# Sample attention rewritten as half-steps that four engines take in program order

## The chip, the cores and the metric

The kernel is one program on one core of a Trainium2 chip. Six queues matter here. PE is the matrix engine (PEld is its loading of weights), DVE, ACT and POOL are the vector, scalar and GpSimd engines, and SP is the queue that issues the transfers between main memory and the core's own memory (SBUF). The metric is the device time of one execution in microseconds (us), as the median of several runs.

## The reference

The reference is one inference step of a two-layer decoder, for a prompt of 1024 tokens and for 8 sample sequences of 8 new tokens each. The change touches one stage of layer 0, the attention of the sample sequences. Each sequence has 2048 cached tokens, in 16 pages of 128 rows that a page table names; a row is a latent vector of 256 numbers and a rotary key of 32. Cut to what matters:

```
def one(args):                      # lax.map over the 8 sample sequences
    c_all  = concat(cached latents (2048 x 256), new latents (8 x 256))
    kr_all = concat(cached rotary keys (2048 x 32), new ones)
    k_nope = rms_norm(einsum('bkc,chd->bkhd', c_all, w_uk), g_k_nope)   # 8 heads x 64
    s = (qn . k_nope + qr . kr_all) * SOFTMAX_SCALE      # masked among the new tokens
    p = softmax(s)                                       # over the 2056 keys
    lat = einsum('bhqk,bkc->bqhc', p, c_all)
    return einsum('bqhc,chv->bqhv', lat, w_uv)
```

Everything is float32. The kernel gets near it by splitting an operand into a rounded high part and a low part (the rest), and using both.

## The kernel before, in words

The program has six stages; the change lies in the third, `sample_attention` (L813 to L1116), which takes about 421 to 787 us of the span. Behind it come the output projection, the multilayer perceptrons and the recurrent layer, which the change leaves as they are.

**One page.** `load` (L826) reads the page's number and issues two transfers on the SP queue: `cp`, the 128 x 256 latents (128 KB, L840), into a ring of 26 buffers, and `kp`, the rotary keys (L841). `transp` (L915) turns two pages at a time: PE transposes them into `cpt`, ACT casts the high part `ch`, DVE takes the low part `cl`. `keys` (L943) makes 12 matmuls into `pk` (L136: six with 256 columns, six with 320). Of the result, ACT squares the keys (`psq`, L954) and copies the 64 raw scores to `s` (L955), and DVE sums the squares per head (`pss`, L956). `ropes` and `ropes2` add the rotary products, `kpt` and `pr`, for four pages at a time.

**Half a sequence (8 pages).** `scale8` (L958) turns the sums of squares into reciprocal roots (`rsqrt`, L109 to L127: `rsx`, a shift `rst`, a first guess `rsr`, then three Newton steps of three operations, all on DVE), multiplies the scores and adds the rotary part.

**One sequence.** `soft0` to `soft3` take the maximum over the keys (`smx`, transposed in `mxt`, `m`, `sdg`, spread by the matmul `mxb`), and then in two halves subtract it (DVE, L999), take the exponent (ACT, L1000), cast it to the weights' high part `ph` (ACT, L1001) and form their low part (DVE, L1002). A reduction `ssm` (DVE, L1004) sums the weights. Then for each page `vsplit` (L1009) splits `cp` into `vh` (ACT) and `vl` (POOL), a ring of four each, and this split is the last reader of the page's `cp` buffer; `latent` (L1018) makes two matmuls into `lat`. `lat3` turns the result, divides by the sum and writes `latT`. The tiles `kpt`, `mxt`, `mxb` and `lo` share one PSUM bank (`msc`, tag "ms").

**What sets the order.** The main loop (L1069) takes two pages at a time. `slot(b - 1, q)` places the softmax and the weighted sum of one sequence between the pages of the next one. The program's order is only a priority, though: the scheduler of the tile framework puts each engine's instructions in the order in which it expects them to become ready. So the first four `vsplit` of a sequence stand far ahead of its softmax, and the first weights of the output projection (`op.weights(0)`, called by `ahead` when 24 pairs of pages are left) are split long before this stage. The semaphores between engines follow from the tiles.

Of the kernel before, what the change touches and what calls it, by code (L numbers as in the profile page):

```python
# [20 lines left out]
P = 128  # L21
# [76 lines left out]

def wcols(g, w, c0, c1, ring):

    return wunit(g, w[:, c0:c1].rearrange("(k p) m -> p k m", p=P), KB, c1 - c0, ring)


def rsqrt(g, out, ss, inv_n, n, p=P):
# [3 lines left out]
    t = g.tiny.tile([P, 64], I32, name="rst", tag="rst")[:p, :n]  # L108
# [13 lines left out]
    v.tensor_single_scalar(t, x.bitcast(I32), 1, ALU.logical_shift_right)  # L122
    v.tensor_scalar(r.bitcast(I32), t, -1.0, float(0x5F3759DF), ALU.mult, ALU.add)
# [142 lines left out]
class OutProj:  # L266
# [47 lines left out]
def in_even(g, I, O, S, st_left):  # L314
# [3 lines left out]
    with ExitStack() as st:  # L318
# [90 lines left out]
        def zproc(ci, tb0, nb, zs, sq):  # L409
# [398 lines left out]
def sample_attention(g, I, S, ahead, fill_start, fill):  # L808
    nc = g.nc
    SQ = H * DT  # L810
    with ExitStack() as st:
# [75 lines left out]
        nc.vector.tensor_copy(i2[NS:], g.ident[NS:, NS:])  # L887
        latT = sa.tile([P, 2, H, NS], F32, name="latT", bufs=1)
# [68 lines left out]

        def scale8(b, g8):  # L958
            ss = ss8[b].rearrange("p a h -> p (a h)")
            r = g.tiny.tile([P, 64], F32, name="prs", tag="prs", bufs=2)  # L960
            rsqrt(g, r, ss, 1.0 / QN, 64)
# [6 lines left out]
        mxs, ph_, sm_, pl_ = {}, {}, {}, {}  # L968
# [22 lines left out]

        def soft3(b, dg):
            s = sc[b]
            pb = msc("mxb")
            nc.tensor.matmul(pb[:, :SQ], g.ones[:SQ], dg[:SQ], start=True, stop=True)
            ph = sa.tile([P, NPG + 1, 2, SQ], F32R, name="ph", tag="ph", bufs=1)
            for x, y in HF:
                sv = s[:, x:y]
                nc.vector.tensor_tensor(sv, sv, pb[:, None, :SQ].to_broadcast([P, y - x, SQ]), ALU.subtract)  # L999
                nc.scalar.activation(sv, sv, AF.Exp, scale=SCALE)  # L1000
                nc.scalar.copy(ph[:, x:y, 0], sv)  # L1001
                nc.vector.tensor_tensor(ph[:, x:y, 1], sv, ph[:, x:y, 0].bitcast(F32), ALU.subtract)  # L1002
# [6 lines left out]
        def vsplit(b, pg):  # L1009
            ch = sa.tile([P, R], F32R, name="vh", tag="vh", bufs=4)  # L1010
            c_l = sa.tile([P, R], F32R, name="vl", tag="vl", bufs=4)
            nc.scalar.copy(ch, cps[b, pg])
            e = nc.vector if b == DB - 1 and pg % 4 else nc.gpsimd
            e.tensor_tensor(c_l, cps.pop((b, pg)), ch.bitcast(F32), ALU.subtract)
            vs[b, pg] = (ch, c_l)

        def latent(b, pg):
# [9 lines left out]
            nc.tensor.matmul(pl[:, :R], w, vh, start=(pg == 0), stop=False)  # L1027
# [4 lines left out]
        def lat2(b):  # L1032
            ls = sa.tile([P, R], F32, name="ls", tag="ls")
            nc.scalar.copy(ls, pl_.pop(b)[:, :R])
            lss[b] = ls

        def lat3(b):
            ls = lss.pop(b)
            po = msc("lo")
            for k in range(2):  # L1040
                nc.tensor.matmul(po[:, k * SQ:(k + 1) * SQ], ls[:, k * P:(k + 1) * P], i2, start=True, stop=True)
            nc.tensor.matmul(po[:, 2 * SQ:3 * SQ], g.ones, sm_.pop(b), start=True, stop=True)
            ri = sa.tile([P, SQ], F32, name="sri", tag="sri")
            nc.vector.reciprocal(ri, po[:, 2 * SQ:3 * SQ])
            for k in range(2):
                nc.vector.tensor_tensor(latT[:, k, :, b * DT:(b + 1) * DT], po[:, k * SQ:(k + 1) * SQ].rearrange("p (h t) -> p h t", t=DT),
                                        ri.rearrange("p (h t) -> p h t", t=DT), ALU.mult)

        def slot(b, q):

            if b < 0:
# [5 lines left out]
            if 3 <= q <= 11:  # L1057
                for pg in range(2 * (q - 3), min(2 * (q - 3) + 2, NPG)):
                    vsplit(b, pg)
            if 5 <= q <= 13:  # L1060
                for pg in range(2 * (q - 5), 2 * (q - 5) + 2):
                    if pg <= NPG:
                        latent(b, pg)
            if q == 13:
                lat2(b)
            if q == 15:
                lat3(b)

        st_ = {}  # L1069
# [4 lines left out]
        for J in range(NJ + 8):  # L1074
            b, pr = divmod(J, 8)
            if J == NJ:
                stk.close()
                fill_start()
            if J < NJ:
                ahead(NJ - J)  # L1080
                if J + 2 < NJ:
                    load(*divmod(J + 2, 8))
                if pr == 0 and b > 0:
                    scale8(b - 1, 1)
                    soft1(b - 1)
                if pr == 4:
                    scale8(b, 0)
                    soft0(b)
# [529 lines left out]
```

## Time and profile before

| what | us |
|---|---|
| median of three runs | 2800.52 (2797.41 to 2801.54) |
| the profiled execution | 2799.98 |
| its span | 2798.1 |
| PE busy | 2694.8 (96%) |
| DVE busy | 1779.9 (64%) |
| ACT busy | 899.4 (32%) |
| POOL busy | 364.4 (13%) |

The span goes from the first to the last instruction. A row of a timeline gives when an instruction began and how long it took, and in brackets how long its engine had been idle before and what released it; an "x4" joins four neighbours that are alike. PE's matmuls overlap, so that their spacing, not their duration, tells what they cost. A clock of 1.00 is TensorE's full 2.4 GHz, 0.50 is 1.2 GHz.

### The profile page before, as it was taken

How to read it: one execution, taken by the hardware profiler on the slowest of the kernel's cores; microseconds unless marked ns; L12 is line 12 of the kernel's file. 1: busy time of each engine (PE TensorE's matmuls, PEld its weight loads, DVE VectorE, ACT ScalarE, POOL GpSimd, SP SyncE). 2: the span in 40 equal slices, each digit the busy share in tenths (PEclk: the TensorE clock that was granted, in tenths of full speed). 3: DMA queues.
4: the chain of work that ended last, by engine and by line, in shares of the span. 5: the costliest groups of instructions: out<-in, count | busy, mean ns of one | idle time of the engine just before them, and what ended most of it. 6: DMA issues, size and time to landing. Idle time of an engine off the chain costs nothing.

```text
span 2798.1 us, 42984 instructions
## 1 busy us (share of the span) xinstructions
PE 2694.8 (96%) x16801; PEld 2612.2 (93%) x16801; DVE 1779.9 (64%) x3477; ACT 899.4 (32%) x1878; POOL 364.4 (13%) x429
## 2 busy tenths in 40 slices
PE   7998999999899999999999999998999999999999
PEld 6887988888889999999999989998999999999998
DVE  7665666888855555555555577996555555555555
ACT  5334555666644111111111135664411111111111
POOL 4221000332322000000000033444200000000000
PEclk9999998999999999999999999999999999999999
DMA  5233103221251111111111111113111111111111
GB/s 156 63 117 109 39 9 80 67 56 50 61 147 51 46 39 49 43 46 46 46 46 46 46 73 45 42 41 110 56 40 45 46 46 46 46 46 46 38 31 65
DMA packets 200742, 162.06 MB, mean 58 GB/s; under 512 B 40331, under 2 KB 183148, under 8 KB 199763
## 3 DMA queue, kind: packets, MB, share of 16 engines
q1 hardware_dynamic: 200539, 159.31, 19.1%
q8 instruction: 133, 2.18, 0.3%
q14 instruction: 70, 0.57, 0.1%
HBM read 138.18 MB, written 21.21 MB: 57 GB/s over the span
## 4 chain that ended last, share of the span: by engine, by line
PE 63%; DVE 7%; ACT 1%; issue 0%; DMA 0%; POOL 0%; ACTq 0%; DVEq 0%; SPq 0%; POOLq 0%
PE up L136 27%; PE dn L136 26%; PE op L136 6%; PE pu L136 2%; DVE xl L182 1%; DVE v L1339 1%; DVE ig L1354 1%; PE pgt L136 1%; DVE hs L1370 0%; DVE t L1355 0%; DVE y L250 0%; DVE ta L1357 0%; DVE xl L80 0%; PE pg L136 0%; DVE ig L1363 0%
## 5 line engine op out<-in xcount | busy, mean ns | idle before, releaser
L250 DVE TENSOR_TENSOR y<-y,dn 128x384 f32<-128x384 f32 (+1 forms) x768 | 404.6, 530 | 281.9 <-PE dn L136 279.8
L136 PE MATMUL dn<-hh,whB 128*128 128x384 f32 (+1 forms) x1536 | 505.7, 329 | 3.9 <-DVE y L250 3.8
L136 PE MATMUL up<-xh,wlA 128*128 128x384 f32 (+1 forms) x1536 | 501.6, 327 | 0.0
L136 PE MATMUL up<-xh,whA 128*128 128x384 f32 (+1 forms) x1536 | 501.1, 326 | 0.0
L136 PE MATMUL dn<-hh,wlB 128*128 128x384 f32 (+1 forms) x1536 | 501.0, 326 | 0.0
L136 PE MATMUL up<-xl,whA 128*128 128x384 f32 (+1 forms) x1536 | 501.0, 326 | 0.0
L136 PE MATMUL dn<-hl,whB 128*128 128x384 f32 (+1 forms) x1536 | 500.6, 326 | 0.0
L79 ACT CAST whB<-raw 128x1024 fp32r<-128x1024 f32 (+3 forms) x80 | 79.9, 1034 | 701.7 <-PE dn L136 663.2
L136 PEld LDWEIGHTS dn<-hh,whB 128*128 128x128 f32 x1536 | 288.3, 188 | 11.8 <-DVE y L250 11.6
L136 PEld LDWEIGHTS up<-xh,wlA 128*128 128x128 f32 x1536 | 288.3, 188 | 0.4
L136 PEld LDWEIGHTS up<-xh,whA 128*128 128x128 f32 x1536 | 288.3, 188 | 0.3
L136 PEld LDWEIGHTS dn<-hl,whB 128*128 128x128 f32 x1536 | 288.4, 188 | 0.1
L136 PEld LDWEIGHTS up<-xl,whA 128*128 128x128 f32 x1536 | 288.3, 188 | 0.2
L136 PEld LDWEIGHTS dn<-hh,wlB 128*128 128x128 f32 x1536 | 288.3, 188 | 0.0
L235 DVE SCALAR_TENSOR_TENSOR rl<-up,rs 128x384 f32<-128x384 f32 (+1 forms) x192 | 102.8, 535 | 260.4 <-PE up L136 260.4
L236 ACT ACTIVATE hh<-rl 128x384 fp32r<-128x384 f32 (+1 forms) x192 | 97.1, 506 | 447.7 <-DVE rl L235 447.7
L136 PE MATMUL pk<-wqh,cl 128*128 128x256 f32 (+1 forms) x512 | 153.3, 305 | 12.7 <-DVE cl L925 12.6
L79 ACT CAST whA<-raw 128x1024 fp32r<-128x1024 f32 (+2 forms) x94 | 98.0, 1043 | 195.1 <-PE up L136 143.2
L136 PE MATMUL pk<-wqh,ch 128*128 128x320 f32 (+1 forms) x512 | 159.8, 314 | 0.7 <-ACT ch L924 0.7
L80 POOL TENSOR_TENSOR wlA<-raw,whA 128x1024 fp32r<-128x1024 f32 (+2 forms) x24 | 58.1, 2422 | 768.6 <-ACT whA L79 768.6
L237 DVE TENSOR_TENSOR rl<-rl 128x384 f32<-128x384 f32 (+1 forms) x192 | 105.9, 552 | 77.5 <-ACT hh L236 77.5
L136 PE MATMUL pk<-wql,ch 128*128 128x256 f32 (+1 forms) x512 | 151.7, 298 | 1.2 <-DVE wql L80 1.2
(556 smaller groups left out, 5272.4 us busy)
## 6 DMA issues: line engine op xcount, KB each, us to landing
raw<-in_w_up_dram SPq DMA_DIRECT2D x64, 512.0 KB
raw<-in_w_down_dram SPq DMA_DIRECT2D x64, 512.0 KB
cp<-in_cache_ckv_dram SPq DMA_DIRECT2D x128, 128.0 KB
raw<-in_w_in_rnn_dram SPq DMA_DIRECT2D x16, 512.0 KB
xt<-in_x_prompt_dram SPq DMA_DIRECT2D x8, 512.0 KB
raw<-in_w_out_even_dram SPq DMA_DIRECT2D x8, 512.0 KB
raw<-in_x_prompt_dram SPq DMA_DIRECT2D x8, 512.0 KB
raw<-in_w_out_rnn_dram SPq DMA_DIRECT2D x8, 512.0 KB
```

The costliest lines, as they stand in the source:

```text
L79: g.nc.scalar.copy(h, src)
L80: (lo or g.nc.vector).tensor_tensor(l, src, h.bitcast(F32), ALU.subtract)
L136: g.nc.tensor.matmul(ps, a, b, start=(i == 0), stop=(i == n - 1))
L182: nc.vector.scalar_tensor_tensor(xl[:, m], yv, gcol[:, m:m + 1], xh[:, m].bitcast(F32), ALU.mult, ALU.subtract)
L235: nc.vector.scalar_tensor_tensor(r[:, :n], ps[:, :n], 0.0, RS[c][:, :n], ALU.max, ALU.mult)
L236: nc.scalar.activation(hh[:, a:b], r[:, :n], AF.Square)
L237: nc.vector.tensor_tensor(r[:, :n], r[:, :n], r[:, :n], ALU.mult)
L250: nc.vector.tensor_tensor(y[c][:, m], y[c][:, m], ps[:, :n], ALU.add)
L1339: V.scalar_tensor_tensor(v, ul[:, a + k:b + k], vec[:, k, n:n + 1], v, ALU.mult, ALU.add)
L1354: V.scalar_tensor_tensor(t2, t2, 1.0, v, ALU.add, ALU.mult)
```

## The change

The change rewrites the stage in five ways.

1. `rsqrt` makes its first guess in one operation, without the shift, and can put its Newton steps on another engine. `scale8`'s root becomes `norm8`: `rsx` and `rsr` on DVE, and then 12 operations on POOL.
2. The sum of the weights comes out of the weighted sum itself. Each `vh` has two columns of ones behind its 256, so that the high matmul of `latent` has 258. The `ssm` reduction, the matmul with ones and the 128 x 64 reciprocal go; `lat3` has a small matmul `lf` and a reciprocal of one column in their place, and `lat4` does the rest.
3. `vh` and `vl` are four fixed pairs of tiles.
4. The loop goes by half-steps of one page, n, and stands under `manual_schedule` for PE, DVE, ACT and POOL: these take their instructions in the order of the program. Of a sequence's 16 half-steps, the next sequence's half-step q carries the softmax: q = 0 the second `norm8`, 2 `scale8`, 5 `mxt`, 6 `mxb` with the first exponent and both subtractions, 7 the second exponent, 7 to 14 `vsplit` of two pages each, 8 to 15 their `latent`. `transp` stands at the start of each even half-step, for the pair of pages that is used two half-steps later; before it stood half a step behind.
5. `ahead` loads the first weights of the output projection at 24 pairs left and splits them (`op.parts`) at 20.

The diff, cut to its core:

```
-def rsqrt(g, out, ss, inv_n, n, p=P):
+def rsqrt(g, out, ss, inv_n, n, p=P, eng=None):
...
-    v.tensor_single_scalar(t, x.bitcast(I32), 1, ALU.logical_shift_right)
-    v.tensor_scalar(r.bitcast(I32), t, -1.0, float(0x5F3759DF), ALU.mult, ALU.add)
+    v.tensor_scalar(r.bitcast(I32), x.bitcast(I32), -0.5, float(0x5F3759DF), ALU.mult, ALU.add)
+    if eng is not None:
+        for it in range(3):
+            eng.tensor_tensor(u, r, r, ALU.mult)
+            eng.tensor_tensor(u, u, x, ALU.mult)
+            eng.tensor_scalar(u, u, -0.5, 1.5, ALU.mult, ALU.add)
+            eng.tensor_tensor(out if it == 2 else r, u, r, ALU.mult)
+        return
...
+        fold = sa.tile([P, 2, NS], F32, name="fold", bufs=1)
+        VT = [(sa.tile([P, R + 2], F32R, name=f"vh{i}", bufs=1), sa.tile([P, R], F32R, name=f"vl{i}", bufs=1)) for i in range(4)]
+        for vh, _ in VT:
+            nc.gpsimd.memset(vh[:, R:].bitcast(F32), 1.0)
...
+        def norm8(b):
+            ss = ss8[b].rearrange("p a h -> p (a h)")
+            r = prs[b] = g.tiny.tile([P, 64], F32, name="prs", tag="prs", bufs=2)
+            rsqrt(g, r, ss, 1.0 / QN, 64, eng=nc.gpsimd)
...
-            sm = sa.tile([P, SQ], F32, name="ssm", tag="ssm")
-            nc.vector.tensor_reduce(sm, s.rearrange("p a q -> p q a"), AX.X, ALU.add)
...
         def vsplit(b, pg):
-            ch = sa.tile([P, R], F32R, name="vh", tag="vh", bufs=4)
-            c_l = sa.tile([P, R], F32R, name="vl", tag="vl", bufs=4)
-            nc.scalar.copy(ch, cps[b, pg])
+            ch, c_l = vs[b, pg] = VT[pg % 4]
+            nc.scalar.copy(ch[:, :R], cps[b, pg])
...
-            nc.tensor.matmul(pl[:, :R], w, vh, start=(pg == 0), stop=False)
+            nc.tensor.matmul(pl[:, :R + 2], w, vh, start=(pg == 0), stop=False)
...
         def lat3(b):
+            pf = msc("lf")
+            nc.tensor.matmul(pf[:, :2], fold.rearrange("p a q -> p (a q)"), lss[b][:, R:], start=True, stop=True)
+            nc.vector.reciprocal(ri, pf[:, 0:1])
+            nc.vector.tensor_scalar_mul(i2s, i2, ri)
...
             if q == 0:
+                norm8(b)
+            elif q == 2:
+                scale8(b, 1)
+            elif q == 3:
+                soft1(b)
+            elif q == 5:
                 st_[b] = soft2(b)
-            elif q == 2:
+            elif q == 6:
                 soft3(b, st_.pop(b))
+                shift(b, 0)
+                weigh(b, 0)
+                shift(b, 1)
+            elif q == 7:
+                weigh_low(b, 0)
+                weigh(b, 1)
+            elif q == 8:
+                weigh_low(b, 1)
...
+            if 8 <= q <= 15:
+                for pg in (2 * q - 16, 2 * q - 15):
+                    latent(b, pg)
+            if 7 <= q <= 14:
+                for pg in (2 * q - 14, 2 * q - 13):
                     vsplit(b, pg)
...
+        with g.tc.manual_schedule(engines={ET.PE, ET.DVE, ET.Activation, ET.Pool}):
+            for n in range(2 * NJ):
+                b, q = divmod(n, 16)
+                if q % 2 == 0:
+                    J = n // 2
+                    ahead(NJ - J)
+                    if J + 2 < NJ:
+                        load(*divmod(J + 2, 8))
+                    if J + 1 < NJ:
+                        transp(*divmod(J + 1, 8))
+                if q % 4 == 3:
+                    kT[b, q // 4] = ropes(b, q // 4)
+                slot(b - 2, q + 16)
+                slot(b - 1, q)
+                if q == 8:
+                    norm8(b)
+                elif q == 10:
+                    scale8(b, 0)
+                elif q == 11:
+                    soft0(b)
+                elif q == 13 and b + 1 < DB:
+                    begin(b + 1)
+                keys(b, q)
...
             if left == 24:
-                op.weights(0)
+                op.load(0)
+            elif left == 20:
+                op.parts()
```

Two places of the order, in the second sequence. The first is PE, where the 27th and 28th page of the stage are transposed; these are the first whose `cp` buffers were used before, by pages 1 and 2. Before, `cp_5910` and `cp_5922` are those pages, and `vh_5948` to `vl_5953` belong to the first sequence's pages 7 and 8:

```order
L136 MATMUL pk_6049<-wql1_4917,ch_5965 128x320
L136 MATMUL pk_6049<-wqh1_4916,cl_5966 128x320
L1027 MATMUL lat_5896<-vh_5948,ph_5760 128x256
L1028 MATMUL lat_5896<-vl_5949,ph_5760 128x256
L1027 MATMUL lat_5896<-vh_5952,ph_5760 128x256
L1028 MATMUL lat_5896<-vl_5953,ph_5760 128x256
L921 MATMUL cpt_6079<-ident_73,cp_5910 128x128 x2
L921 MATMUL cpt_6079<-ident_73,cp_5922 128x128 x2
L136 MATMUL pk_6088<-wqh1_4916,ch_5965 128x256
L136 MATMUL pk_6088<-wql1_4917,ch_5965 128x256
```

After, `cp_5861` and `cp_5873` are the 27th and 28th page, and `vh0` to `vl1` hold the first sequence's pages 1 and 2:

```order
L158 MATMUL pk_5923<-wql1_4892,ch_5803 128x320
L158 MATMUL pk_5923<-wqh1_4891,cl_5804 128x320
L957 MATMUL cpt_5966<-ident_73,cp_5861 128x128 x2
L957 MATMUL cpt_5966<-ident_73,cp_5873 128x128 x2
L1074 MATMUL lat_5976<-vh0_4919,ph_5887 128x258
L1075 MATMUL lat_5976<-vl0_4920,ph_5887 128x256
L1074 MATMUL lat_5976<-vh1_4921,ph_5887 128x258
L1075 MATMUL lat_5976<-vl1_4922,ph_5887 128x256
L158 MATMUL pk_6004<-wqh1_4891,ch_5881 128x256
L158 MATMUL pk_6004<-wql1_4892,ch_5881 128x256
```

The transposes moved ahead of the first two latents' matmuls, where before eight pages' stood ahead of them.

The second is POOL, at the first sequence's end. Before, `vl_5801` to `vl_5857` are the splits of its pages 1 to 4, `vl_5889` and on those behind them, and `s<-snew` copies the scores of the new tokens for a sequence's softmax:

```order
L900 AFFINE_SELECT msk_5089<-msk_5089 64x64
L1014 TENSOR_TENSOR vl_5801<-cp_4813,vh_5800 128x256
L1014 TENSOR_TENSOR vl_5805<-cp_4825,vh_5804 128x256
L1014 TENSOR_TENSOR vl_5853<-cp_4837,vh_5852 128x256
L1014 TENSOR_TENSOR vl_5857<-cp_4849,vh_5856 128x256
L978 COPY s_4948<-snew_4943 64x64
L977 MEMSET s_5578 64x64
L978 COPY s_5578<-snew_4943 64x64
L977 MEMSET s_6343 64x64
L978 COPY s_6343<-snew_4943 64x64
L1014 TENSOR_TENSOR vl_5889<-cp_4968,vh_5888 128x256
L1014 TENSOR_TENSOR vl_5893<-cp_4980,vh_5892 128x256
```

After, pages 1 to 4 are `cp_4788` to `cp_4824`, and `rsu_5987` is the root of the second sequence's first half:

```order
L1018 MEMSET s_4937 64x64
L1019 COPY s_4937<-snew_4932 64x64
L1062 TENSOR_TENSOR vl0_4920<-cp_4788,vh0_4919 128x256
L1062 TENSOR_TENSOR vl1_4922<-cp_4800,vh1_4921 128x256
L1062 TENSOR_TENSOR vl2_4924<-cp_4812,vh2_4923 128x256
L1062 TENSOR_TENSOR vl3_4926<-cp_4824,vh3_4925 128x256
L141 TENSOR_TENSOR rsu_5987<-rsr_5988 128x64
L142 TENSOR_TENSOR rsu_5987<-rsu_5987,rsx_5986 128x64
L143 TENSOR_SCALAR rsu_5987<-rsu_5987 128x64
L144 TENSOR_TENSOR rsr_5988<-rsu_5987,rsr_5988 128x64
```

The four splits moved from ahead of the copy of the scores to behind it, and the root's operations, which DVE had, stand behind them and ahead of the next splits.

## Rows read from the trace of the kernel before

**Rows 1.** Windows: us; busy (count) of PE, PEld, DVE, ACT, POOL; clock, DMA share, GB/s.

```profile
517.30:558.80 41.50, 38.95 (x282) 36.22 (x281) 34.43 (x67) 26.51 (x84) 12.21 (x18) 1.00 0.23 58
```

**Rows 2.** Waits, 475.4 to 762 us: total us, times, longest us.

```profile
POOL vl L1014 <- ACT vh L1012: 178.9, 34, 22.8
...
PEld pk L136 <- DVE cl L925: 16.6, 23, 2.7
PE pk L136 <- DVE cl L925: 12.0, 10, 2.5
...
PEld lat L1028 <- POOL vl L1014: 7.4, 15, 0.9
```

**Rows 3.** Timeline of PE: start us, us, engine, line, operation [idle before].

```profile
560.38 0.28 PE L136 MATMUL pk<-wqh,ch 128*128 128x256 f32 x1
...
561.99 0.60 PE L921 MATMUL cpt<-ident,cp 128*128 128x128 f32 x4
...
564.02 0.28 PE L136 MATMUL pk<-wqh,ch 128*128 128x256 f32 x1
...
581.14 0.28 PE L1027 MATMUL lat<-vh,ph 128*128 128x256 f32 x1
581.26 0.28 PE L1028 MATMUL lat<-vl,ph 128*128 128x256 f32 x1
```

**Rows 4.** DVE in the steady part, then in the last sequence (timeline), then grouped lines.

```profile
528.14 1.34 DVE L999 TENSOR_TENSOR s<-s,mxb 128x512 f32<-128x512 f32 x2
...
536.34 2.93 DVE L122 TENSOR_SCALAR rst<-rsx 128x64 int32<-128x64 int32 x1
...
763.55 0.18 DVE L122 TENSOR_SCALAR rst<-rsx 128x64 int32<-128x64 int32 x1
...
781.75 1.23 DVE L1014 TENSOR_TENSOR vl<-cp,vh 128x256 fp32r<-128x256 f32 x3 [0.41 <-ACT vh L1012]
...
L1004 DVE TENSOR_REDUCE ssm<-s 128x64 f32<-128x1088 f32 x7 | 14.8, 2117 | 0.0
```

**Rows 5.** Timeline of ACT in one softmax.

```profile
529.29 0.62 ACT L1000 ACTIVATE s<-s 128x512 f32<-128x512 f32 x1
...
531.41 0.69 ACT L1001 CAST ph<-s 128x576 fp32r<-128x576 f32 x1
...
532.11 0.71 ACT L1012 CAST vh<-cp 128x256 fp32r<-128x256 f32 x2
```

**Rows 6.** POOL: timeline, then one grouped line (busy us, mean ns).

```profile
255.30 2.36 POOL L80 TENSOR_TENSOR wlA<-raw,whA 128x1024 fp32r<-128x1024 f32 x1 [23.55 <-ACT whA L79]
...
420.42 0.28 POOL L899 TENSOR_SCALAR_AFFINE_SELECT msk<-msk 64x64 f32<-64x64 f32 x1
420.77 0.28 POOL L900 TENSOR_SCALAR_AFFINE_SELECT msk<-msk 64x64 f32<-64x64 f32 x1
...
508.38 1.44 POOL L1014 TENSOR_TENSOR vl<-cp,vh 128x256 fp32r<-128x256 f32 x2 [0.86 <-ACT vh L1012]
532.60 2.63 POOL L1014 TENSOR_TENSOR vl<-cp,vh 128x256 fp32r<-128x256 f32 x3 [22.77 <-ACT vh L1012]
...
L1396 POOL TENSOR_TENSOR y<-q,hs 128x64 f32<-128x64 f32 x8 | 3.9, 488 | 0.0
```

**Rows 7.** Page loads: timeline of the SP queue, and windows around the first.

```profile
533.36 0.33 SPq L840 DMA_DIRECT2D cp<-in_cache_ckv_dram  x1
...
534.46 0.33 SPq L840 DMA_DIRECT2D cp<-in_cache_ckv_dram  x1
...
533.30:534.40 1.10, 0.96 (x7) 0.71 (x5) 1.10 (x2) 1.10 (x4) 1.10 (x3) 1.00 0.00 1
534.40:535.40 1.00, 0.30 (x3) 0.12 (x2) 1.00 (x3) 1.00 (x5) 0.94 (x2) 1.00 0.48 147
```

**Rows 8.** Clock in the last sequence: PE timeline, and the window behind it.

```profile
770.20 0.66 PE L1174 MATMUL xtp<-ident,raw 128*128 128x128 f32 x2 [2.19 <-DMA raw<-in_x_prompt_dram]
...
769.40:776.10 6.70, 5.90 (x26) 5.45 (x27) 2.60 (x6) 3.55 (x7) 0.00 (x0) 0.50 0.50 171
```

More of the change, by code (lines that the diff above doesn't have):

```diff
@@ L96, in wunit, with wload, wparts @@
     return v[1], v[2]
+def wload(g, w, c0, c1):
+    raw = raw_tile(g)[:, :1024]
+    g.nc.sync.dma_start(raw.rearrange("p (a b) -> p a b", b=c1 - c0), w[:, c0:c1].rearrange("(k p) m -> p k m", p=P))
+    return raw
+def wparts(g, raw, ring):
+    pl, nb = g.ring[ring]
+    wh = pl.tile([P, 1024], F32R, name="wh" + ring, tag="wh" + ring, bufs=nb)
+    wl = pl.tile([P, 1024], F32R, name="wl" + ring, tag="wl" + ring, bufs=nb)
+    split(g, wh, wl, raw, g.lo)
+    return tuple(t.rearrange("p (a b) -> p a b", a=KB) for t in (wh, wl))
 def wcols(g, w, c0, c1, ring):
     return wunit(g, w[:, c0:c1].rearrange("(k p) m -> p k m", p=P), KB, c1 - c0, ring)
-def rsqrt(g, out, ss, inv_n, n, p=P):
+def rsqrt(g, out, ss, inv_n, n, p=P, eng=None):
     v = g.nc.vector
     x = g.tiny.tile([P, 64], F32, name="rsx", tag="rsx")[:p, :n]
-    t = g.tiny.tile([P, 64], I32, name="rst", tag="rst")[:p, :n]
     u = g.tiny.tile([P, 64], F32, name="rsu", tag="rsu")[:p, :n]
@@ L276, in weights, with load, parts @@
             self.ws[m] = wcols(self.g, self.w, m * P, (m + 1) * P, self.rings[m])
+    def load(self, grp):
+        self.raw = {m: wload(self.g, self.w, m * P, (m + 1) * P) for m in self.GROUPS[grp]}
+    def parts(self):
+        for m, raw in self.raw.items():
+            self.ws[m] = wparts(self.g, raw, self.rings[m])
     def chunk(self, grp, c):
@@ L966, in scale8 @@
             nc.vector.tensor_tensor(sf, sf, pr8[b].rearrange("p a q -> p (a q)"), ALU.add)
-        mxs, ph_, sm_, pl_ = {}, {}, {}, {}
+        mxs, ph_, pl_ = {}, {}, {}
         HF = ((0, 8), (8, NPG + 1))
@@ L1043, in lat3 @@
[L1043 to L1047, printed above, removed]
+                nc.tensor.matmul(po[:, k * SQ:(k + 1) * SQ], ls[:, k * P:(k + 1) * P], i2s, start=True, stop=True)
@@ new lines, in slot @@
+                shift(b, 1)
[4 more added lines that the diff above has]
+                weigh_low(b, 1)
+            elif q == 16:
+                latent(b, NPG)
+                lat2(b)
+            elif q == 17:
+                lat3(b)
+            elif q == 20:
+                lat4(b)
+            if 8 <= q <= 15:
[3 more added lines that the diff above has]
+                for pg in (2 * q - 14, 2 * q - 13):
+                    vsplit(b, pg)
@@ L1073, in sample_attention @@
         NJ = DB * 8
[L1074 to L1086, printed above, removed]
+        ET = mybir.EngineType
+        with g.tc.manual_schedule(engines={ET.PE, ET.DVE, ET.Activation, ET.Pool}):
[15 more added lines that the diff above has]
+                elif q == 10:
                     scale8(b, 0)
+                elif q == 11:
                     soft0(b)
[L1089 to L1092 removed]
+                elif q == 13 and b + 1 < DB:
+                    begin(b + 1)
+                keys(b, q)
+                if n == 2:
                     new_keys()
[L1094 to L1106 removed]
+                if q % 4 == 0 and n:
+                    bb, qq = divmod(n - 4, 16)
+                    ropes2(bb, qq // 4, kT.pop((bb, qq // 4)))
+            ropes2(DB - 1, 3, kT.pop((DB - 1, 3)))
+        stk.close()
+        fill_start()
+        for q in range(21):
+            slot(DB - 2, q + 16)
+            slot(DB - 1, q)
         fill()
```

85 lines of the change are left out of this document (34 added, 51 removed).

## The prediction

> **What bounds the kernel now.** I read the page first: PE is busy for 96% of the span, but over all stages, so I went to the windows of single sequences. A steady sequence takes 41.5 us, and in it PE is busy for 38.95 us, DVE for 34.4, ACT for 26.5 and POOL for 12.2, at full clock [rows 1]. PE bounds the stage, with small gaps. The list of waits names them: 28.6 us on DVE's low part `cl`, 7.4 on POOL's `vl`, from 475 to 762 us, 6.9 sequences [rows 2]; that is some 5.2 us a sequence. PE's own floor from its timeline: a page's 12 matmuls take 1.61 us, a page with the transposes of two 2.03 [rows 3], so 8 x 3.64 = 29.1; 34 latent matmuls at 0.12 are 4.1 [rows 3]; the rotary, maximum and output matmuls are what remains of 41.5 - 5.2 = 36.3, some 3.1. I take a floor of 36.5.
>
> Why is `cl` late? DVE's timeline shows it: `rst`, a 128 x 64 shift that takes 0.18 us in the last sequence, takes 2.93 in the steady part [rows 4], and meanwhile POOL is splitting pages [rows 6]. `cl` queues behind it.
>
> Two more views matter for what replaces this. POOL waits up to 22.8 us for the next `vh` [rows 2], since four pages of the next sequence are split as soon as the ring is free (508.38) and the fifth only when the weights are there (532.60) [rows 6]. And a page load follows the split that frees its buffer: one is issued at 533.36, 0.76 us after the first of three splits began at 532.60 [rows 6, 7].
>
> **Part by part.** All of it is in the steady sequences, in the starting and last ones, and in `op.parts`.
>
> *Less work on DVE.* Per sequence `ssm` (2.1 us [rows 4]), `rst` and the Newton steps go from an engine that isn't the bound. What they are worth is the 5.2 us of PE's waits; with `cl` made two half-steps ahead they can go entirely. The extra columns of the latents lie between 256 and 320 columns, which PE passes in 0.12 us [rows 3] and (1.61 - 6 x 0.12)/6 = 0.15. I take nothing; up to 17 x 0.03 = 0.5 us a sequence.
>
> *New wait 1, the page ring.* PE's order now has the transposes of pages 27 and 28 (the sequence's pages 11 and 12) at the start of half-step 8, in front of the latents. Their loads need the buffers of the former sequence's pages 1 and 2, and these are released by `vl0` and `vl1` of half-step 7. I follow one sequence from its first page, t = 0. `mxt` waits for POOL's root (see below) and for the shared bank, 0.5 us; PE begins half-step 6 at 13.3, and `mxb` comes out at about 14.4. Behind `cl`, DVE makes the two subtractions in 1.34 us [rows 4], until 16.55. The bank is free only then, so `kpt` of half-step 7 waits 0.9 us, and PE ends half-step 7 at 16.55 + 1.75 = 18.3. ACT, strictly in order, casts the first half until 17.2, squares and copies a page (1.1 us), and then takes the second exponent and cast at 0.69 each [rows 5], until 19.7; then `vh0`, `vh1` at 0.36 each [rows 5], until 20.1 and 20.4. POOL's pair takes 1.44 [rows 6]: `vl0` ends at 20.8, `vl1` at 21.5. The load of page 27 is issued at 20.8, that of 28 1.1 later (533.36, 534.46); nothing moves for 1.0 us after an issue, and 128 KB at 147 GB/s take 0.9 [rows 7], so page 28 lands at 23.9. PE has stood since 18.3: a stall of 5.6, from 4.5 (splits and issues that overlap better) to 6.5. Before, these splits stood at 508.38, ahead of the weights that the one at 532.60 waited for [rows 6]. Queued behind the waiting transposes are the latents and the page's matmuls, so nothing fills the gap.
>
> *New wait 2, the root on POOL.* It is 12 dependent operations on 128 x 64. The trace has no such one in SBUF on an idle POOL; a 64 x 64 select takes 0.28 and its dependent successor begins 0.07 later, and a 128 x 64 product has a mean of 0.49 [rows 6]. 12 x 0.35 = 4.2 from below, 12 x 0.56 = 6.7 from above; I take 4.3, the nearer to the select, since the products' mean lies in a stage where DVE is busy beside them. In half-step 8 it stands between `vl3` and the next four splits: `vl3` ends at 26.2, the root at 30.8, and `vl4`, `vl5` at 32.3. PE, from 24.3 on, makes pages 8 and 9 and reaches the latents of half-step 10 at 29.1: a stall of 3.2, from 1.5 to 5.5. The other root, in half-step 0, is covered by five half-steps of matmuls, to within the 0.5 above.
>
> The Trainium skill speaks here against the change. GPSIMD Engine Reference, section "Engine selection", puts two-input elementwise work on VectorE, since GpSimd is about 2x slower. The trace agrees for the split: 0.41 us on DVE [rows 4] against 0.72 on POOL [rows 6]. By twice DVE's pace the root would take about 5.5, which would add 1.2 a sequence, 8 in all, and make it 2845.
>
> *Sum of a sequence.* 36.5 + 0.5 + 0.9 + 5.6 + 3.2 = 46.7, against 41.5: +5.2. Of the eight sequences, the first has no former one; seven make +36.4.
>
> *The first sequence* has `new_keys` in front of its third page in the strict order, and `kpt` in order: +1, between -1 and +4 from the same half-steps.
>
> *`op.parts`* puts two ACT casts and two POOL splits of 2.36 us [rows 6] into half-step 8 of the sixth sequence, where POOL and ACT are late already: 2 x 2.36 less what the load stall hides, +2, between 0 and 4. Before, they were made at 255 us, beside other work.
>
> *The end* loses `ssm` (2.1) and has its root on POOL as well; PE waits there for loads of `x_prompt` too [rows 8], which hide part of either. I take -2, between -4 and +2.
>
> Sum: 36.4 + 1 + 2 - 2 = +37.4, on 2799.98 of the profiled execution (span 2798.1), which is 0.5 below the median of the runs: **2837**.
>
> **The rivals.**
>
> *A, the pipeline works as drawn.* If splits and loads come in time, only the floor and the bank's 1.4 us are left: 37.9, 3.6 less than before, and seven such sequences with the same +1 give -24: 2776. For it: PE's 5.2 us of waits, and DVE's load, which falls by 2.1 of `ssm` and 3.1 of two `rst` [rows 4] and the Newton steps besides. Against it: page 28 would have to land 5.6 us earlier. It decides if `vl1` ends by about 16 instead of 21.5, which needs ACT or POOL to take the splits ahead of the second exponent; the order forbids it.
>
> *B, only one of the two new waits holds.* If the root on POOL is hidden (faster, or begun in the load's gap), a sequence takes 43.5: +2.0 x 7 + 1 = 2815. If only the root's wait holds, it takes 41.1, and the sum is within 2 us of before.
>
> *C, the clock falls.* In the last sequence PE idled 2.19 us, and the window behind it has a granted clock of 0.50 [rows 8], 1.2 GHz. The new gap of 5.6 is longer. At half clock two pages cost 2 x 1.61 = 3.2 us more; much of it disappears in the wait of half-step 10 that follows. If it doesn't, 1.5 to 3 us a sequence are added: 2848 to 2858. Against it: one wait among many, in a stage that was at 1.00 [rows 1].
>
> **How the numbers follow.** A measurement of this kernel can tell about 0.2%, 5.6 us, from no change. The forecast (2824 to 2850 for its own bounds) has a chance of 0.50, C 0.14, B 0.17 with the root hidden and 0.05 with only the root, A 0.14. Faster are A and none else, 0.14; the same is 0.05, the root alone; slower the rest, 0.81. The range leaves out A at the low end and the last of C and of the bounds at the high end: 2804 to 2862.
>
> **What would show it.** In the changed kernel's windows a steady sequence should take 45 to 48 us, with the same PE work. The waits should have PE `cpt` on the page load with 5 to 6 us, seven times, and `lat` on POOL `vl` with about 3 us, seven times; the waits for `cl` should be gone; POOL's root should take about 4.3 us and SP's loads should wait for `vl0` and `vl1`. If `cpt` doesn't wait, the forecast is wrong in its largest term; if sequences take 37 to 38 us, A holds. A clock under 1.00 from half-step 8 on would be C.

## The result and the profile after

The changed kernel takes 2844.79 us (median; 2839.01 to 2849.84) against 2801.03 for the kernel before in the same job: a ratio of 1.0161, with a 95% interval of 1.0148 to 1.0173. It is slower, by 43.8 us. The forecast was 2837, slower, by way of two new waits in each sequence. Both are in the trace. The profiled execution has a span of 2842.0 us.

The windows of the third and fourth sequence, with the columns of [rows 1], and then the waits of all later sequences:

```profile
515.68:566.26 50.58, 42.38 (x282) 40.00 (x280) 27.55 (x46) 26.45 (x84) 20.03 (x42) 0.90 0.18 48
566.26:615.61 49.35, 41.41 (x282) 39.05 (x280) 27.56 (x46) 26.47 (x85) 20.04 (x43) 0.93 0.18 49
```

```profile
PEld cpt L957 <- DMA cp<-in_cache_ckv_dram: 36.0, 14, 4.4
PE cpt L957 <- DMA cp<-in_cache_ckv_dram: 31.8, 14, 4.1
POOL rsu L141 <- DVE rsr L138: 27.1, 11, 4.2
...
PEld lat L1075 <- POOL vl L1062: 19.9, 17, 2.6
PE lat L1075 <- POOL vl L1062: 16.6, 14, 2.4
```

A sequence took 41.5 us [rows 1] and takes 50.6 and 49.4 here. PE's 12 matmuls a page are the same; DVE is busy for 27.6 us where it was 34.4, and POOL for 20.0 where it was 12.2. The waits for `cl` [rows 2] are gone. In their place PE waits for page loads (`cpt`), 31.8 us, and for POOL's `vl`, 16.6 us, over seven sequences. The granted clock is 0.90 and 0.93, where it was 1.00 (the third figure from the end).

PE's timeline in the third sequence has both waits in their places, half-step 8 and half-step 10:

```profile
529.20 0.30 PE L969 MATMUL kpt<-ident,kp 128*128 128x128 f32 x1 [0.57 <-PE pk L158]
...
530.79 0.31 PE L158 MATMUL pk<-wqh,cl 128*128 128x320 f32 x1
535.11 0.44 PE L957 MATMUL cpt<-ident,cp 128*128 128x128 f32 x2 [4.01 <-DMA cp<-in_cache_ckv_dram]
536.17 0.69 PE L957 MATMUL cpt<-ident,cp 128*128 128x128 f32 x2 [0.63 <-DMA cp<-in_cache_ckv_dram]
...
545.35 0.39 PE L1075 MATMUL lat<-vl,ph 128*128 128x256 f32 x1 [2.36 <-POOL vl L1062]
...
546.48 0.58 PE L1075 MATMUL lat<-vl,ph 128*128 128x256 f32 x1 [0.63 <-POOL vl L1062]
```

It idles from 531.1 to 535.1 and again for 0.6 us until the second page is there, and behind `lat<-vh` it stands 2.36 and 0.63 us. What it waits for is on ACT, POOL and SP:

```profile
530.44 0.72 ACT L1048 ACTIVATE s<-s 128x576 f32<-128x576 f32 x1
531.19 0.67 ACT L1049 CAST ph<-s 128x576 fp32r<-128x576 f32 x1
531.77 0.70 ACT L1060 CAST vh<-cp 128x256 fp32r<-128x256 f32 x2
```

```profile
533.05 0.34 SPq L870 DMA_DIRECT2D cp<-in_cache_ckv_dram  x1
...
534.17 0.33 SPq L870 DMA_DIRECT2D cp<-in_cache_ckv_dram  x1
```

```profile
532.30 1.41 POOL L1062 TENSOR_TENSOR vl<-cp,vh 128x256 fp32r<-128x256 f32 x2 [12.15 <-issue]
537.86 1.95 POOL L1062 TENSOR_TENSOR vl<-cp,vh 128x256 fp32r<-128x256 f32 x2 [4.15 <-ACT vh L1060]
540.18 0.29 POOL L141 TENSOR_TENSOR rsu<-rsr 128x64 f32<-128x64 f32 x1 [0.36 <-DVE rsr L138]
...
544.29 0.32 POOL L144 TENSOR_TENSOR prs<-rsu,rsr 128x64 f32<-128x64 f32 x1
544.57 3.23 POOL L1062 TENSOR_TENSOR vl<-cp,vh 128x256 fp32r<-128x256 f32 x4
```

The second exponent and its cast come first on ACT, then `vh` at 531.77, `vl` at 532.30, the page loads at 533.05 and 534.17, and the transposes at 535.11 and 536.17. The root is on POOL from 540.18 to 544.6, 12 operations in 4.4 us, in front of the next splits. What these waits do to the clock:

```profile
531.68:533.68 2.00, 0.00 (x0) 0.00 (x0) 0.62 (x1) 1.45 (x6) 1.38 (x2) 1.00 0.00 0
535.68:537.68 2.00, 1.51 (x7) 1.51 (x8) 0.17 (x1) 0.78 (x2) 0.00 (x0) 0.50 0.10 21
543.20:545.40 2.20, 0.05 (x1) 0.06 (x1) 1.76 (x3) 0.90 (x3) 1.95 (x6) 1.00 0.00 0
546.50:552.00 5.50, 5.50 (x24) 5.46 (x25) 1.67 (x3) 1.64 (x6) 2.29 (x4) 0.50 0.39 103
```

Each time PE has been idle for 2 us and more (531.68 and 543.20), the clock stands at 0.50 soon after the matmuls resume: for 2 us and more behind the first wait, for 5.5 and more behind the second. Not every sequence shows two such falls. From the second to the seventh the mean clock is 0.89, 0.90, 0.93, 0.93, 0.93 and 0.90, and in the fifth and the sixth it falls once only.

The first copy of scores (`s<-pk`) on ACT marks where a sequence begins. By these marks the 43.9 us between the two spans divide so: the prompt attention and the set-up of the stage -10.8, the first sequence +1.2, the seven others +53.7 (286.5 to 340.2, up to the copy of the last page), the end -1.3; the remaining +1.1 lies ahead of 243 us, in a part with no edit.

### The profile page after: what moved, and what is told of

Its sections match the earlier page's. It is cut to its first block, busy times and chain, and to the rows that moved or that the text cites. A ratio compares the mean times of both kernels' runs of the same rounds, so it can differ in the third digit from the quotient of the medians.

```text
span 2842.0 us, 42942 instructions
## 1 busy us (share of the span) xinstructions
PE 2707.4 (95%) x16801; PEld 2627.9 (92%) x16801; DVE 1724.3 (61%) x3300; ACT 898.4 (32%) x1878; POOL 425.6 (15%) x627
## 4 chain that ended last, share of the span: by engine, by line
PE 62%; DVE 7%; ACT 1%; issue 0%; DMA 0%; POOL 0%; ACTq 0%; DVEq 0%; POOLq 0%; SPq 0%
PE up L158 26%; PE dn L158 26%; PE op L158 6%; PE pu L158 2%; DVE xl L204 1%; PE pgt L158 1%; DVE v L1411 1%; DVE hs L1442 1%; DVE ig L1426 1%; DVE y L272 0%; DVE t L1427 0%; DVE xl L80 0%; PE pg L158 0%; DVE ig L1435 0%; DVE ta L1429 0%
## 5 line engine op out<-in xcount | busy, mean ns | idle before, releaser
L992 DVE TENSOR_REDUCE pss<-psq 128x8 f32<-128x512 f32 x128 | 87.6, 685 | 132.1 <-ACT psq L990 132.0
L158 PE MATMUL pk<-wqh,ch 128*128 128x256 f32 (+1 forms) x512 | 165.6, 323 | 0.0
L158 PE MATMUL pk<-wql,ch 128*128 128x256 f32 (+1 forms) x512 | 158.5, 310 | 0.0
```

Of the source, the lines that this page charges most:

```text
L158: g.nc.tensor.matmul(ps, a, b, start=(i == 0), stop=(i == n - 1))
L992: nc.vector.tensor_reduce(ss8[b][:, pg % 8], sq.rearrange("p f (h d) -> p (f h) d", d=QN), AX.X, ALU.add)
```

## The experiments

The first four ran beside each other, and so did the next four, the next two and the last two. All times are medians of four runs, or ten for e6 and e8; "a sequence" is the mean of the third to the fifth in the profiled execution.

| kernel | total, us | ratio to before (95%) | a sequence, us |
|---|---|---|---|
| before | 2797 to 2801 | | 41.5 |
| after | 2844.8 | 1.0148 to 1.0173 | 49.1 |
| e1, early splits | 2818.6 | 1.0049 to 1.0082 | 45.3 |
| e2, root on DVE | 2815.5 | 1.0037 to 1.0070 | 44.6 |
| e3, both | 2778.2 | 0.9905 to 0.9938 | 39.6 |
| e4, weights early | 2854.0 | 1.0169 to 1.0203 | 48.9 |
| e5, e3 + weights at half-steps 2, 4 | 2773.6 | 0.9895 to 0.9928 | 39.6 |
| e6, order free | 2793.5 | 0.9976 to 0.9995 | 41.2 |
| e7, PE filled | 2828.4 | 1.0092 to 1.0126 | 47.4 |
| e8, before with the new first guess | 2799.8 | 0.9992 to 1.0015 | 42.1 |
| e9, e5 + bank | 2774.3 | 0.9893 to 0.9935 | 39.6 |
| e10, order free, root on DVE | 2763.0 | 0.9856 to 0.9899 | 37.3 |
| e11, e10 + weights late | 2756.2 | 0.9833 to 0.9866 | 37.6 |
| e12, e10 + ssm | 2766.7 | 0.9875 to 0.9912 | 37.7 |

One caution for the few microseconds: up to the first `ptp` of the prompt attention, where no edit reaches, the profiled executions differ by up to 5 us (239.1 in e7, 244.1 in e3). There the column of sequences decides. The kernel before came out at 2797 to 2801 in the jobs, so a difference between kernels of different jobs is good to some 4 us.

**e1: the splits of the first four pages early.**

```
-            if 7 <= q <= 14:
+            if 1 <= q <= 4:
+                vsplit(b, q - 1)
+            if 9 <= q <= 14:
                 for pg in (2 * q - 14, 2 * q - 13):
                     vsplit(b, pg)
```

> The changed kernel, with the splits of a sequence's first four pages moved from half-steps 7 and 8 to half-steps 1 to 4; all else as in the changed kernel. Theory (page ring): the transposes of half-step 8 no longer wait for the page loads (31.8 us of PE's waits now, 4 to 5 a sequence), and the half clock behind that wait goes too; the root on POOL still holds the latents of half-step 10, for about 1.7 us. A sequence falls from 48.9 to about 40, the total to about 2785 (2770 to 2800). Rival (strict order): the stage pays for the strict order of ACT and PE as such, and the wait comes back at the latents of half-step 8 or 10 behind the second exponent; then the total stays above 2825.

The total falls by 26.2 us, a sequence to 45.3. No row of waits has `cpt` on a load any more: the page ring was the cause. But PE now comes to half-step 10 earlier, and finds the root still there. PE in the fourth sequence:

```profile
579.96 0.38 PE L1075 MATMUL lat<-vl,ph 128*128 128x256 f32 x1 [2.85 <-POOL vl L1062]
...
581.09 0.58 PE L1075 MATMUL lat<-vl,ph 128*128 128x256 f32 x1 [0.63 <-POOL vl L1062]
```

```profile
PE lat L1075 <- POOL vl L1062: 28.4, 14, 7.2
```

The wait is 2.85 and 0.63 us, not the 1.7 that I expected, and the clock of that sequence 0.96. The theory holds on the first wait; its number failed on the second, which took 28.4 us of PE over the seven sequences, up from 16.6. Of these, 7.5 us are in the sixth, where `op.parts` stands on POOL as well.

**e2: the root on DVE.** In `norm8` the argument `eng=nc.gpsimd` goes:

```
-            rsqrt(g, r, ss, 1.0 / QN, 64, eng=nc.gpsimd)
+            rsqrt(g, r, ss, 1.0 / QN, 64)
```

> The changed kernel, with the Newton steps of the sample attention's root back on DVE (9 operations in place of POOL's 12), in the same place of the order. Theory: the wait of half-step 10's latents on vl (16.6 us in all, 2 to 3 a sequence) goes, and with it the half clock behind it (up to 3 us in some sequences); the wait on the page loads stays at 4 to 5 us. Total 2815 (2805 to 2830). Rival (the page ring alone matters, the second wait only takes up slack that the first leaves): the total stays within 6 us of 2845.

29.3 us less, as expected:

```profile
PE cpt L957 <- DMA cp<-in_cache_ckv_dram: 32.5, 14, 4.1
PE lat L1075 <- POOL vl L1062: 1.3, 3, 0.5
```

PE waits 1.3 us for `vl` in all, and 32.5 for the loads, as much as before this edit. The rival falls: the second wait is not slack that the first leaves.

**e3: both.**

> Both edits together: first four splits at half-steps 1 to 4, Newton steps on DVE. Theory: neither wait is left, a sequence takes 37.9 (36.5 of matmuls and 1.4 for the shared bank) at full clock, total 2770 (2760 to 2785), below the kernel before. Rival (strict order, or the columns of ones, cost by themselves): a sequence stays above 41.5 and the total above 2800.

66.6 us less than the changed kernel, more than the two alone together (55.4), and 22.6 below the kernel before:

```profile
545.20:584.79 39.59, 38.01 (x282) 36.08 (x280) 31.25 (x65) 26.14 (x84) 12.24 (x18) 1.00 0.25 64
624.40:668.87 44.47, 40.13 (x282) 37.56 (x280) 34.52 (x65) 27.38 (x86) 17.44 (x20) 0.96 0.28 80
```

The clock is at 1.00 again: without the two waits, and the clock behind them, the change is no longer slower than what it replaced. A sequence takes 39.6, not 37.9: PE waits 0.80 us at `mxt`, 0.55 at `kpt` and 0.23 at the first latent, and the 38.0 that are left are more than the floor that I took. Of these, e10 shows 37.3; for the other 0.7 no run shows a cause. The second row is the sixth sequence, the one with `op.parts`: 4.9 us longer.

**e4: the weights split as early as before.**

```
+        ahead(99)
         begin(0)
...
-            if left == 24:
-                op.load(0)
-            elif left == 20:
-                op.parts()
+            if left == 99:
+                op.weights(0)
```

> The changed kernel, with the first weights of the output projection loaded and split where the kernel before does it (about 255 us, at the head of the prompt attention) in place of the sixth sequence. Theory: these transfers and splits delay the prompt attention there, which in the changed kernel ends 6.7 us earlier; the total rises by 6 to 7 us to about 2851. Rival (they are free there, as the prediction took it, and cost 2 us in the sixth sequence): 2843.

9.2 us more. In the profiled executions the stretch from 243 us to the first page is 8.0 us longer. The reason stands in ACT's and PE's timelines; of the kernel before, of the changed one and of e4:

```profile
254.18 1.04 ACT L79 CAST whA<-raw 128x1024 fp32r<-128x1024 f32 x1 [6.08 <-DMA raw<-in_w_out_even_dram]
255.13 1.00 ACT L753 ACTIVATE p<-s,nmx 128x896 f32<-128x896 f32 x1
...
256.27 1.75 PE L764 MATMUL ptp<-ident,p 128*128 128x128 f32 x7 [5.87 <-ACT p L753]
```

```profile
250.22 1.01 ACT L783 ACTIVATE p<-s,nmx 128x896 f32<-128x896 f32 x1 [0.81 <-DVE nmx L781]
```

```profile
254.23 1.04 ACT L79 CAST whA<-raw 128x1024 fp32r<-128x1024 f32 x1 [5.37 <-DMA raw<-in_w_out_even_dram]
255.18 1.00 ACT L783 ACTIVATE p<-s,nmx 128x896 f32<-128x896 f32 x1
```

ACT takes its work in order, and the cast of a weight that is still on its way stands in front of the exponents: 6.08 us of waiting, and PE idle for 5.87 behind it. In the changed kernel the exponent of 255.13 begins at 250.22.

**e5: the same weights, in e3, one each at half-steps 2 and 4 of the sixth sequence.**

```
-            elif left == 20:
-                op.parts()
+            elif left in (23, 22):
+                op.parts(23 - left)
```

> Early splits and Newton steps on DVE, as in the run before, and the split of the output projection's first weights moved from half-step 8 of the sixth sequence to its half-steps 2 and 4 (one weight each), where POOL has little to do. Theory: that sequence took 44.5 us where its neighbours take 39.6, with 2.4 us of PE's wait on vl behind POOL's 5.2 us of weights and a half clock after it; it falls to 39.6, the total from 2778 to 2773. Rival (the splits cost what they cost, wherever they stand): 2778.

The total is the theory's, the reason isn't. In the profiled execution the sixth sequence still takes 44.8 us; what is gained lies in the stretch ahead of 240 us (239.6 here, 244.1 in e3). Against the kernel before of its own job, e5 is 24.1 us faster and e3 22.6, so that only some 1.5 of the 4.6 us are left. The rival holds. PE now waits 4.17 us at `mxt`, behind DVE. DVE and POOL, in order of time:

```profile
624.42 1.91 DVE L1005 TENSOR_TENSOR s<-s,prs 128x512 f32<-128x512 f32 x1
...
628.09 2.34 POOL L80 TENSOR_TENSOR wlA<-raw,whA 128x1024 fp32r<-128x1024 f32 x1
...
628.77 2.42 DVE L1022 TENSOR_TENSOR smx<-smx 128x64 f32<-128x64 f32 x1
```

A maximum of 128 x 64 with two inputs takes 0.22 us where POOL is idle (747.83), 0.81 beside a page's split of 0.74 (547.87), and 2.42 beside POOL's split of a weight, and then ends 0.8 us behind it. The product ahead of it takes 1.91 in place of 0.68. The Trainium skill states this for such operations (SBUF — State Buffer, section "Who interferes with whom"): a VectorE instruction with two SBUF inputs contends with a GpSimd instruction that reads SBUF. The trace agrees, with 2.42 us against 0.22.

**e6: the order left to the scheduler.** `with nullcontext():` stands in place of `manual_schedule`.

> The changed kernel without manual_schedule: the program and its arithmetic as changed, the order of PE, DVE, ACT and POOL left to the framework's scheduler, as before the change. Theory: the scheduler hoists the first four splits as it did before, PE no longer waits for page loads, and what is left is the root on POOL; a sequence takes 40 to 44 us, the total 2780 to 2815. Rival (the lost time lies in the new operations, not in the order): above 2830.

51.3 us less than the changed kernel with the same operations, just below the kernel before: the rival falls, the order it was. What is left of the waits is the root on POOL, by another way:

```profile
DVE s L1005 <- POOL prs L144: 54.2, 14, 5.1
...
PEld cpt L957 <- DVE cl L961: 24.2, 14, 2.5
PE cpt L957 <- DVE cl L961: 20.6, 14, 2.2
```

DVE waits 54.2 us for the root, and PE 20.6 us for `cl`, before it can write the transposes' bank again. With the root on DVE (e10) DVE no longer waits for it, nor PE for `cl`.

**e7: PE kept busy in the waits.**

```
             pt = one("cpt", "ct").rearrange("p (a b c) -> p a b c", a=2, b=2)
+            for _ in range({5: 40, 6: 28}.get(pr, 0) if b > 0 else 0):
+                nc.tensor.transpose(pt[:, 0, 0], cps[b, pr * 2 - 1][:, :P], g.ident)
```

> The changed kernel with 40 extra transposes (into the bank that the page's transposes then overwrite) ahead of half-step 8's page transposes, and 28 ahead of half-step 10's, from the second sequence on: work without use, that keeps PE busy where it waits for the page loads (4 us) and shortly before it waits for vl. All else waits as in the changed kernel. Theory (the clock is a cost of its own, besides the waits): the granted clock of a sequence rises from 0.90-0.93 to 0.98 or more and a sequence falls from 48.9 to about 46.5, the total by 12 to 20 us to 2825-2833. Rival (the waits' length is all, the slow matmuls are absorbed in the next wait, as the prediction had it): within 6 us of 2845, or above it by the extra transposes.

16.4 us less, though 68 transposes more stand in each sequence:

```profile
509.14:556.65 47.51, 45.87 (x350) 43.65 (x348) 27.27 (x46) 26.51 (x85) 20.14 (x43) 1.00 0.18 49
556.65:603.97 47.32, 45.87 (x350) 43.64 (x348) 27.30 (x46) 26.52 (x85) 20.14 (x43) 1.00 0.19 51
```

```profile
524.41 4.53 PE L956 MATMUL cpt<-ident,cp 128*128 128x128 f32 x40
...
528.77 0.38 PE L959 MATMUL cpt<-ident,cp 128*128 128x128 f32 x2
```

```profile
PE cpt L959 <- DMA cp<-in_cache_ckv_dram: 4.0, 7, 0.8
...
PE lat L1077 <- POOL vl L1064: 2.9, 13, 0.8
```

The clock is 1.00 throughout, and a sequence takes 47.4 where it took 49.1. Of the total, 4.5 us lie ahead of 243 us (239.1 against 243.6); the seven sequences give 11.7 (328.5 against 340.2), 1.7 each. The theory holds in its kind: the fall of the clock is a cost of its own and not all absorbed. By size it is under the 2.4 expected, since the extra transposes don't all fit into the waits: 40 of them take 4.36 us, 68 take 7.4, and PE's two waits were 6.9 a sequence (31.8 and 16.6 in seven) and are 1.0. From this what the clock had cost can be estimated. Seven times 7.4 us of transposes, less the 41.5 us by which the waits fell, would have been some 10 us more; 11.7 less were measured. So the clock had cost some 22 us, 3.1 a sequence.

**e8: the kernel before with the new first guess alone.**

```
-    v.tensor_single_scalar(t, x.bitcast(I32), 1, ALU.logical_shift_right)
-    v.tensor_scalar(r.bitcast(I32), t, -1.0, float(0x5F3759DF), ALU.mult, ALU.add)
+    v.tensor_scalar(r.bitcast(I32), x.bitcast(I32), -0.5, float(0x5F3759DF), ALU.mult, ALU.add)
```

> The kernel before, with one edit of the change alone: rsqrt's first guess in one operation, without the shift. Theory (the shift is blocked for 2.9 us by POOL's splits, and any one-input DVE operation in its place is blocked likewise): the block moves to the next such operation, and the time falls by 0 to 4 us (2797 to 2801). Rival (the shift itself is what makes cl late): PE's waits on cl, some 4 us a sequence, go, and the time falls by 20 us or more, to 2780.

No change that can be measured in the total. The block has moved, as the theory has it: `rsx`, 0.13 us where POOL is idle, is now the long one, beside POOL's splits, and PE's waits for `cl` stay: 17.8 us, where they were 12.0 [rows 2]. POOL and DVE, in order of time:

```profile
536.09 2.12 POOL L1012 TENSOR_TENSOR vl<-cp,vh 128x256 fp32r<-128x256 f32 x3
...
536.70 1.56 DVE L114 TENSOR_SCALAR rsx<-pss 128x64 f32<-128x64 f32 x1
...
558.02 0.13 DVE L114 TENSOR_SCALAR rsx<-pss 128x64 f32<-128x64 f32 x1
```

In the profiled execution a sequence is 0.6 longer, and that is the clock. The third and the fourth:

```profile
518.34:559.48 41.14, 38.17 (x282) 36.08 (x281) 33.94 (x65) 26.22 (x84) 11.73 (x18) 1.00 0.23 59
559.48:602.19 42.71, 39.73 (x282) 37.63 (x281) 33.97 (x65) 26.32 (x84) 11.71 (x18) 0.96 0.22 57
```

The work is the same and PE's waits are too (2.97 and 2.98 us), but one sequence stands at 1.00 and the other at 0.96, and it takes 1.6 us more. The sequences of e6 split likewise: 40.2 us at 1.00, 41.7 to 41.8 at 0.96.

**e9: e5 with two moves against the waits for the bank.** `lat4` stands at q = 18, and the second `kpt` and its product at half-steps 8 and 9:

```
-            elif q == 20:
+            elif q == 18:
                 lat4(b)
...
-                if q % 4 == 3:
+                if q % 4 == 3 and q != 7:
                     kT[b, q // 4] = ropes(b, q // 4)
...
                 if q == 8:
+                    kT[b, 1] = ropes(b, 1)
                     norm8(b)
...
-                if q % 4 == 0 and n:
+                if q % 4 == 0 and q != 8 and n or q == 9:
```

> The kernel of e5 (early splits, Newton steps on DVE, weights split at half-steps 2 and 4) with two more moves against the waits for the shared bank: lat4 one half-step behind lat3 (q = 18 in place of 20), so that latT is copied before the maximum's transpose, and the second kpt of a sequence and its product one half-step later (8 and 9 in place of 7 and 8), behind the subtraction that frees the bank. Theory: PE's 0.8 us at mxt and 0.55 at kpt go, a sequence falls from 39.6 to 38.3, the total by 7 to 10 us to about 2765. Rival (the waits turn up one half-step later): 2771 to 2775.

A sequence stays at 39.6: the rival holds. In the steady sequences PE's waits at `mxt` and `kpt` are gone, and over all sequences 7.7 us at the latents, on ACT's `ph`, and 4.0 at `lo`, on DVE's `i2s`, have come. The sixth sequence alone falls, to 41.4.

**e10: order free, root on DVE.** The edits of e2 and e6 together.

> The changed kernel without manual_schedule (as e6) and with the Newton steps on DVE: the program as changed, the order free, POOL without the root. Theory (the strict order is worth something by itself, once its waits are mended): the free order stays above e3's 2778, at 2785 to 2800. Rival (the strict order is worth nothing; what made e3 fast are the lighter operations): 2778 or less.

The rival holds: the strict order, mended (e3), costs 15 us against the free one.

```profile
543.22:580.54 37.32, 37.19 (x282) 36.03 (x280) 30.28 (x64) 26.32 (x85) 12.22 (x18) 1.00 0.24 63
580.54:617.85 37.31, 37.20 (x282) 36.03 (x280) 30.29 (x64) 26.32 (x85) 12.22 (x18) 1.00 0.26 68
```

PE is busy for 37.19 of 37.32 us, and its timeline there has not one row with an idle time. This is the floor of the changed kernel's work.

**e11: e10 with the weights' transfers held back to the sixth sequence.**

```
-                    ahead(NJ - J)
+                    with g.tc.issue_after(dmas[-1]) if NJ - J == 24 else nullcontext():
+                        ahead(NJ - J)
```

> The kernel of e10 (free order, Newton steps on DVE), with the transfers of the output projection's first weights held back until the page loads of the sixth sequence have been issued, so that the scheduler cannot put the weights' split ahead of the prompt attention. Theory: ACT's wait of some 6 us for these transfers at about 250 us goes, and in the sixth sequence the two splits cost 0 to 4 us: total 2756 to 2760. Rival (what is gained there is lost in the sixth sequence): 2763 or more.

6.8 us less than e10, and the fastest: 43.0 us below the kernel before, a ratio of 0.9849 (0.9833 to 0.9866). In the profiled execution the stretch from the first `ptp` to the first page is 7.2 us shorter than in e10, and the sequences that take the splits are 1.0 and 0.4 us longer.

**e12: e10 with the `ssm` reduction back, its result unused.**

```
+            sm = sa.tile([P, SQ], F32, name="ssm", tag="ssm", bufs=1)
+            nc.vector.tensor_reduce(sm, sc[b].rearrange("p a q -> p q a"), AX.X, ALU.add)
```

> The kernel of e10 with the ssm reduction of the weights put back on DVE (2.1 us a sequence), its result unused; the sum still comes from the columns of ones. Theory (DVE's work is on the path of the softmax, and each of its microseconds there counts): 7 to 15 us more, 2770 to 2778. Rival (with the order free DVE has room for it): within 3 us of 2763.

3.7 us more than e10, but 1.4 when each is taken against the kernel before of its own job, and 0.4 a sequence in the profiled executions, some 3 in all. That is at the edge of the rival and far below the theory. DVE has room for 2.1 us; of the 34 us between before and e10, the reduction is a tenth at most.

## Why the prediction was right, and where it was not

The side and the mechanism are as forecast: the two waits came where they were named, and taking both away (e3) takes the loss away. Two terms were mis-sized, and they offset each other: the seven sequences cost 17.3 us more than forecast, and the time ahead of them, where the splits of `op.parts` no longer stand, fell by 10.8, where `op.parts` was forecast to add 2. That the time came within 8 us is so in part luck.

*New wait 1, the page ring: right.* 5.6 us forecast, 4.01 + 0.63 = 4.6 measured in the third sequence and 4.5 in the mean of seven, by the chain that was named: second exponent, cast, `vh`, `vl`, issue, landing. e1 takes this wait away, and the other one grows. The first load went out 0.75 us after the first split began, as [rows 7] had it.

*New wait 2, the root on POOL: right.* The root takes 4.4 us against 4.3 forecast; the wait is 2.36 + 0.63 = 3.0 against 3.2, and 2.4 in the mean of seven. e2 takes it away.

*The clock, rival C: the term that failed by size.* The prediction said that most of it "disappears in the wait of half-step 10 that follows". In the fifth sequence part of it did: there the clock falls behind the first wait alone, and the wait for `vl` is 1.4 us, where the third has 3.0. But four of the six sequences from the second to the seventh have a second fall behind the wait of half-step 10, and no wait stands behind that to take it up. A sequence takes 49.0 in the mean of these six; 37.9 of work and bank and 6.8 of the two waits leave 4.3, and 3.6 if the work is taken as 38.6 (38.0 in e3, and 0.57 at `kpt`). e7 gives 3.1. All of these lie above C's 1.5 to 3, and the forecast's own sum took the clock at nothing. e8's sequences show 1.6 us for a mean clock of 0.96 in place of 1.00, where the changed kernel has 0.89 to 0.93. So the seven sequences cost 53.7 us more and not 36.4, although both waits were shorter than forecast.

*`op.parts`: the step that was wrong.* "Before, they were made at 255 us, beside other work": they were not beside it but in front of it, and a row of before (254.18, above) would have told. Forecast was +2, measured by e4 about -8; for the other 2.8 us of the -10.8 in that stretch no run shows a cause. The cost of 0 to 4 us in the sixth sequence is not to be seen in the changed kernel (48.5 us, its neighbours 47.4 and 49.5), why is not shown; it is 4.9 in e3, where the two waits are gone.

*The floor and the bank.* 36.5 and 1.4 were forecast. The floor is 37.3 (e10); in the changed kernel the bank costs 0.57 at `kpt` and nearly nothing at `mxt`. The sum is 37.9 in both.

*Less work on DVE.* The `cl` waits went, as forecast. But the 5.2 us a sequence count twice, since the rows of [rows 2] for PE and for its weight loads overlap: all that stands between the kernel before and the floor is 41.5 - 37.3 = 4.2, and PE's idle times in a sequence of the kernel before are 2.2 to 2.4.

*The pace of GpSimd.* By the rule of the Trainium skill that GpSimd takes twice as long (GPSIMD Engine Reference, section "Engine selection"), the root was estimated at 5.5 us. Measured are 0.29 to 0.32 us for a two-input operation of 128 x 64, against 0.23 on DVE: for so small a tile the ratio is 1.3 to 1.4, and the root took 4.4. That the 2845 of that estimate is the measured total is chance.

The totals of e10, e6, e2 and the changed kernel put the causes in a square. Strict order instead of free costs 52.5 us with the root on DVE and 51.3 with it on POOL; the root on POOL instead of DVE costs 29.3 us in the strict order and 30.5 in the free one. The two causes add up, as far as the caution above lets it be said. What of the strict order's price is not the late splits (e3 against e10, 15 us) has been seen only as waits for the bank that moved when they were pushed (e9). It is 22 us against e11, which like e3 splits the weights in the sixth sequence; e10's total holds the delay at 255 us that e3 does not have. Open stays also what makes e10 faster than the kernel before by 34 us: the first guess is worth nothing (e8), the reduction 1 to 4 (e12), and the earlier transposes and the half-step slots were not tried by themselves.

## What to carry to other kernels

A buffer ring ties the end of one step to the start of another: before moving the last reader of a buffer later, count which load needs it, and add issue and landing to the split that frees it. Each of these engines takes its work in order, whether a hand or a scheduler made that order, and an operation that waits in it holds all behind it: the cast of data on its way, which the scheduler had put in front of the exponents, cost PE 5.87 us, and the root on POOL, put in front of the splits by hand, 2.4 a sequence. And price an idle time of PE of some microseconds with the clock that follows it, which here came to some 3 to 4 us a sequence on 6.9 of waits.

## What the runs showed of the hardware

PE's clock fell to 0.50 behind waits of 2.4 to 4 us in the midst of a busy stage, and stayed there for 2 to over 5.5 us. It did not fall behind each: in e8 two sequences with the same work and the same waits stood at 1.00 and 0.96, and took 41.1 and 42.7 us. Filled with transposes without use, the waits left it at 1.00, and seven sequences became 11.7 us faster by doing more.

A DVE operation beside a POOL split can take as long as the split: 2.42 us for a 128 x 64 maximum (0.22 alone), and 1.56 for a 128 x 64 `tensor_scalar` (0.13 alone). The chain of 12 dependent 128 x 64 operations on POOL paces at 0.37 us each.
